# Two blocks of a transformer on one core: which modulation slabs TensorE multiplies directly

## The chip, the cores and the metric

The kernel runs on one core of one Trainium2 chip. The metric is the device time of one execution in microseconds (us), the median of several runs. The core has five engines, each with its own in-order instruction stream: TensorE (PE in the rows, with its weight loads as PEld), VectorE (DVE), ScalarE (ACT), GpSimd (POOL) and SyncE (SP). SP issues most of the DMAs here, one after the other.

## The reference, cut to what matters

Two transformer blocks follow each other on 512 tokens of width 1024. Only the start of the first block matters for the change: a condition vector `c` is turned into six modulation vectors by the matrix `w_ada` (1024 x 6144, float32), the tokens are normalised, scaled and shifted by the first two of them, and multiplied by `w_in`.

```
mod = silu(c) @ w_ada[l] + b_ada[l]
shift1, scale1, gate1, shift2, scale2, gate2 = split(mod, 6)
h = rms_norm(x, norm1_g[l]) * (1.0 + scale1) + shift1
z = h @ w_in[l]
c_q, c_kv, k_pe, dq, dk, dv = split(z, offsets)
```

What comes after is two kinds of attention (low-rank "mla" heads and differential heads), an output projection, a mixture of 32 experts, and then the second block: a convolution, sparse attention, cross attention and a feed-forward layer. The change touches none of these.

## The kernel before, in words

Products that need float32 accuracy are made of three matmuls (lines 84 to 86, the helper `mm3`): a matrix is split into a rounded high part and the low rest, and high x high, high x low and low x high are summed. A weight therefore passes through three steps: a DMA into a tile `raw`, a copy on ScalarE into `whi`, a subtraction on VectorE into `wlo` (line 100, or line 372 in the stage of the change).

**The start stage** (`phase_a1`, inside `tc.manual_schedule()`) runs in exactly the order in which it is written. The 512 tokens are normalised and transposed into `xT`, eight feature blocks of 128. Then the work comes in two halves of four feature blocks. For each half the kernel needs the matching 512 columns of shift1 and of scale1, that is `silu(c)` times a 1024 x 1024 part of `w_ada`. The class `Modulation` computes that from eight slabs of 128 rows and 1024 columns, 512 KB each. A slab can go one of two ways:

```
    def step(self):
        ...
        if k in self.direct:
            self.matmuls(w, g, k == ND - 1)
        elif k == 0:
            v.tensor_scalar(self.acc, w, g, None, op0=OP.mult)
        else:
            v.scalar_tensor_tensor(self.acc, w, g, self.acc, op0=OP.mult, op1=OP.add)
        if k == self.last:
            self.matmuls(self.acc, self.K.ones[:, 0:1], k == ND - 1)
```

On the VectorE way (lines 148 and 150) the slab is scaled by its part of `silu(c)` and added to the accumulator `acc`; once the last such slab is in, eight matmuls with a column of ones (line 137) sum `acc` over its rows. On the direct way the same eight matmuls of line 137 take the slab itself as weights and the column of `silu(c)` (`cs`) as the one moving column. Each of the eight float32 matmuls loads 128 x 128 weights, moves one column, and stands as two rows in the profile, so a slab or an accumulator makes 16 rows. All of them add into one PSUM tile `modb`, from which VectorE makes the factors `mod` (lines 377 and 379). ScalarE then scales and shifts `xT` into `hh` (lines 385 and 386), VectorE makes the rest `hl` (387), and TensorE multiplies with the slab of `w_in` (`products`, 48 matmuls for each half, into four PSUM tiles `pz`). In the first half slabs 1 and 4 are direct, in the second none.

The slabs of `w_ada` share eight buffers, so slab k of the second half is fetched into the buffer of slab k of the first half once that has been read. SP issues all DMAs in the written order; an issue that waits holds up everything behind it.

**After the start stage** the order is no longer the written one: a scheduler in the framework places the instructions of `a_proj` (the other columns of `w_in`, the rope products of line 229, and four more modulation vectors through `Gates.steps`, all on the VectorE way) and of the attention behind it on each engine. It does that with its own estimate of when each is ready, so a change in the start stage can shift the order there too.

Of the kernel before, what the change touches and what calls it, by code (L numbers as in the profile page):

```python
# [19 lines left out]
S, D, P = 512, 1024, 128  # L20
# [301 lines left out]
def phase_a1(K, pp, ps, pst, wp, pm, cols, gates):  # L322

    tc, nc, A = K.tc, K.nc, K.A
    T = {}
    w_in = A["w_in"][0]
# [11 lines left out]
    with tc.tile_pool(name="a_h", bufs=1, reuse_waits="tile") as ph:  # L338
        hh = ph.tile([P, ND, S], F32R, name="hh")
        hl = ph.tile([P, ND, S], F32R, name="hl")  # L340
        with tc.tile_pool(name="a_norm", bufs=1, reuse_waits="tile") as pn, tc.manual_schedule():
# [14 lines left out]
            def turned(t, x):  # L356
                for g in range(2):
                    pt = pst.tile([P, 4, P], F32, tag="tr", name=K.uid("tr"))
                    for j in range(4):
                        f = 4 * g + j  # L360
                        nc.tensor.transpose(pt[:, j, :], x[:, f * P:(f + 1) * P], K.ident)
                    nc.scalar.activation(xT[:, 4 * g:4 * g + 4, t * P:(t + 1) * P], pt, AF.Copy)

            def slab(n):
                raw = wp.tile([P, 4, 512], F32, tag="raw", bufs=2, name=K.uid("raw"))
                nc.sync.dma_start(raw, w_in[512 * n:512 * n + 512, 0:512].rearrange("(k p) c -> p k c", p=P))
                return (wp.tile([P, 4, 512], F32R, tag="whi", name=K.uid("whi")),
                        wp.tile([P, 4, 512], F32R, tag="wlo", name=K.uid("wlo")), raw)

            def part(w, k):  # L370
                nc.scalar.activation(w[0][:, k], w[2][:, k], AF.Copy)
                nc.vector.tensor_tensor(w[1][:, k], w[2][:, k], w[0][:, k].bitcast(F32), op=OP.subtract)
# [22 lines left out]
            wada = A["w_ada"][0].rearrange("r (s c) -> r s c", c=512)  # L395
            pz = [ps.tile([P, 512], F32, tag="sc" if t else "mm", name=K.uid("pz")) for t in range(NT)]
            xs = [scaled(0), scaled(1)]
            for t in range(NT):
                if t < 2:
                    xs.append(scaled(t + 2))  # L400
                turned(t, xs[t])
            mod = Modulation(K, pm, pm, ps, gates.cs, wada[:, 0:3:2], (1, 4))
            for k in range(ND):
                mod.step()
            w = slab(0)
            for k in range(3):
                part(w, k)
            m = factors(0, mod)
            part(w, 3)
            mod = Modulation(K, pm, pm, ps, gates.cs, wada[:, 1:4:2])  # L410
            for q in range(4):
                mod.step()
                modulated(0, q, m)
# [2 lines left out]
            for k in range(4):  # L416
                mod.step()
            products(0, 3, w)
            w = slab(1)
            for k in range(3):  # L420
                part(w, k)
# [5 lines left out]
            raw = wp.tile([P, ND, 2, 64], F32, tag="raw", bufs=2, name=K.uid("raw"))  # L427
# [9 lines left out]
        with tc.tile_pool(name="a_proj", bufs=2, reuse_waits="tile") as wk:  # L437
# [9 lines left out]
            for t in range(NT):  # L447
                for j in range(2):
                    c = slice(256 * j, 256 * j + 256)
# [145 lines left out]
def phase_a(K, R, ctx, st_b, dpool, modd):  # L595
    tc, nc, A = K.tc, K.nc, K.A
    with ExitStack() as st:
        ps = st.enter_context(tc.tile_pool(name="a_ps", bufs=3, space=PSUM))
        pst = st.enter_context(tc.tile_pool(name="a_pst", bufs=2, space=PSUM))
        with ExitStack() as sm:  # L600
            sq = ExitStack()
            with tc.tile_pool(name="a_pp", bufs=1) as pp:
                cols, cs = condition(K, pp, pst)
                lam_init = 0.8 - 0.6 * math.exp(-0.3 * 0)
                with tc.tile_pool(name="a_w", bufs=2, side="right", reuse_waits="tile") as wp:
                    with tc.tile_pool(name="a_mod", bufs=1, side="right", reuse_waits="tile") as pmod:
                        gates = Gates(K, pmod, ps, pst, cs, cols, modd)
                        T = phase_a1(K, pp, ps, pst, wp, pmod, cols, gates)
                    lam = mix_lambda(K, pp, lam_init)
                    pa = sq.enter_context(tc.tile_pool(name="a_qk", bufs=1, reuse_waits="tile"))  # L610
                    vecd = phase_up(K, T, pa, ps, wp, gates, dpool)
                pm = sm.enter_context(tc.tile_pool(name="a_mix", bufs=1, side="right", reuse_waits="tile"))
                mh = pm.tile([P, ND, S], F32R, name="mh")
                ml = pm.tile([P, ND, S], F32R, name="ml")
                router = router_weights(K, pm, ps)
                with tc.tile_pool(name="a_raw", bufs=1, side="right", reuse_waits="tile") as pr:
                    w_first = load_w(K, pm, A["w_out"][0], 0, 256, rawpool=pr, rawbufs=1, bufs=2)
                    phase_a2(K, T, mh, ml, ps, pst, lam, lam_init)
                sq.close()
# [1335 lines left out]
```

## Time and profile before

| | us |
|---|---|
| median of 3 runs | 1976.5 (1974.02 to 1979.04) |
| profiled execution | 1976.37 |
| its span, first to last instruction | 1974.6 |
| PE busy in it | 1908.5 (97%) |
| DVE busy | 1096.4 (56%) |
| ACT busy | 768.9 (39%) |
| mean DMA rate over the span | 181 GB/s |

The shares are means over stages with different limits. In the first 44 us, where the change is, PE is far from 97% busy and the DMA engines run at about 390 GB/s. The chain that ended last is PE work for 48% of the span, mostly the three matmuls of `mm3`.

### The profile page before, as it was taken

What the parts mean: (1) busy time and instruction counts of PE and PEld (TensorE: products, weight loads), DVE (VectorE), ACT (ScalarE), POOL (GpSimd) and SP (SyncE); (2) the same over time, 40 slices, a digit from 0 to 9 for tenths busy, and PEclk for the clock granted to TensorE, in tenths of its full rate; (3) what the DMA queues carried; (4) which work ended last, traced back from release to release, by engine and by line L of the source; (5) the groups of instructions that cost most, each with busy time, mean ns of one, the idle gap of its engine ahead of it and who ended that gap; (6) DMA issues with size and microseconds to landing.
All of it is one profiled execution on the core that took longest, in us unless ns stands there. A gap on an engine that the chain in (4) does not pass through costs nothing.

```text
span 1974.6 us, 26494 instructions
## 1 busy us (share of the span) xinstructions
PE 1908.5 (97%) x10338; PEld 1395.7 (71%) x10338; DVE 1096.4 (56%) x1963; ACT 768.9 (39%) x1602; POOL 148.7 (8%) x215
## 2 busy tenths in 40 slices
PE   6998998899999999979999999999999999999998
PEld 5786678545445454448777777777898898888886
DVE  6976653732332223356999989747555544444423
ACT  5435653321112211123336776786344443333321
POOL 0110000000000000001011001101100001111000
PEclk8999999899999999989999999999999999999999
DMA  9845045699999999953332222202342133333322
GB/s 309 313 170 144 1 179 191 236 408 403 420 415 416 416 420 415 399 155 100 96 107 64 55 54 65 54 22 75 96 130 85 44 91 96 100 96 97 126 78 86
DMA packets 212919, 356.89 MB, mean 181 GB/s; under 512 B 18519, under 2 KB 163283, under 8 KB 188216
## 3 DMA queue, kind: packets, MB, share of 16 engines
q1 hardware_dynamic: 210432, 348.91, 49.2%
q0 software_dynamic: 2096, 6.17, 1.0%
q8 instruction: 83, 1.36, 0.3%
q14 instruction: 44, 0.36, 0.1%
q10 hardware_dynamic: 264, 0.10, 0.0%
HBM read 350.88 MB, written 9.49 MB: 183 GB/s over the span
## 4 chain that ended last, share of the span: by engine, by line
PE 48%; DVE 5%; issue 1%; ACT 1%; DMA 0%; POOL 0%; DVEq 0%; POOLq 0%; SPq 0%; ACTq 0%
PE pz L86 13%; PE pz L84 13%; PE pz L85 13%; PE po L1653 3%; PE tr L1647 2%; DVE cva L1472 2%; DVE wlo L100 1%; PE sc L1623 1%; PE sc L1624 1%; PE pm L934 1%; PE po L1638 0%; PE tr L1297 0%; DVE q L241 0%; DVE K L251 0%; DVE p L1626 0%
## 5 line engine op out<-in xcount | busy, mean ns | idle before, releaser
L84 PE MATMUL pz<-hh,whi 128*128 128x512 f32 x912 | 362.7, 398 | 1.3 <-DVE cblk L1366 0.8
L86 PE MATMUL pz<-hh,wlo 128*128 128x512 f32 x912 | 360.0, 395 | 0.8 <-DVE wlo L100 0.8
L85 PE MATMUL pz<-hl,whi 128*128 128x512 f32 x912 | 359.2, 394 | 0.0
L99 ACT ACTIVATE whi<-raw 128x1024 fp32r<-128x1024 f32 (+2 forms) x166 | 181.1, 1096 | 350.6 <-PE pz L85 265.7
L100 DVE TENSOR_TENSOR wlo<-raw,whi 128x1024 fp32r<-128x1024 f32 (+2 forms) x166 | 219.6, 1326 | 81.7 <-ACT whi L99 81.2
L1070 PE MATMUL eg<-ew,xg 128*64 128x512 f32 x1024 | 224.3, 593 | 0.0
L84 PEld LDWEIGHTS pz<-hh,whi 128*128 128x128 f32 x912 | 171.4, 188 | 37.8 <-issue 2.1
L86 PEld LDWEIGHTS pz<-hh,wlo 128*128 128x128 f32 x912 | 171.4, 188 | 37.2 <-issue 2.1
L85 PEld LDWEIGHTS pz<-hl,whi 128*128 128x128 f32 x912 | 171.4, 188 | 35.3 <-issue 2.5
L1472 DVE SCALAR_TENSOR_TENSOR cva<-cv,cvp,cva 128x512 f32<-128x512 f32 x240 | 179.1, 757 | 4.2
L1070 PEld LDWEIGHTS eg<-ew,xg 128*64 128x64 f32 x1024 | 72.7, 137 | 142.3 <-issue 137.0
L1102 PE MATMUL ey<-ew,hT 128*64 128x512 f32 x512 | 115.1, 603 | 0.7 <-ACT hT L1091 0.7
L1107 DVE TENSOR_TENSOR yg<-ey,gate 128x512 f32<-128x512 f32 x32 | 22.1, 691 | 125.6 <-PE ey L1102 123.7
L1102 PEld LDWEIGHTS ey<-ew,hT 128*64 128x64 f32 x512 | 35.7, 138 | 70.7 <-issue 68.9
L991 ACT ACTIVATE xg<-px,norm2s 128x128 f32<-128x128 f32 x128 | 48.1, 456 | 90.3 <-PE px L986 90.3
L1108 ACT ACTIVATE yh<-yg 128x512 fp32r<-128x512 f32 x32 | 20.2, 630 | 156.4 <-DVE yg L1107 156.4
L1628 ACT ACTIVATE p<-p,am 128x128 f32<-128x128 f32 (+3 forms) x128 | 71.0, 559 | 19.6 <-DVE am L1626 16.6
L1626 DVE CUSTOM_DVE_ANT_0 p<-sc,bias 128x128 f32<-128x128 f32 (+3 forms) x128 | 59.8, 486 | 29.7 <-PE sc L1624 19.0
L1644 ACT ACTIVATE p<-p,am 128x128 f32<-128x128 f32 (+3 forms) x128 | 64.1, 554 | 13.4 <-DVE am L1634 13.1
L84 PE MATMUL pz<-whi,gh 128*128 128x512 f32 x176 | 68.5, 389 | 0.0
L85 PE MATMUL pz<-wlo,gh 128*128 128x512 f32 x176 | 68.5, 389 | 0.0
L86 PE MATMUL pz<-whi,gl 128*128 128x512 f32 x176 | 68.5, 389 | 0.0
(487 smaller groups left out, 3572.4 us busy)
## 6 DMA issues: line engine op xcount, KB each, us to landing
ew<-in_w_expert_gate_dram SPq DMA_DIRECT2D x64, 1024.0 KB
ew<-in_w_expert_up_dram SPq DMA_DIRECT2D x64, 1024.0 KB
ew<-in_w_expert_down_dram SPq DMA_DIRECT2D x64, 1024.0 KB
raw<-in_w_in_dram SPq DMA_DIRECT2D x53, 512.0 KB
wada<-in_w_ada_dram SPq DMA_DIRECT2D x48, 512.0 KB
raw<-in_ffn_in_w_dram SPq DMA_DIRECT2D x44, 512.0 KB
raw<-in_ffn_out_w_dram SPq DMA_DIRECT2D x22, 512.0 KB
raw<-in_w_in_dram SPq DMA_DIRECT2D x8, 1024.0 KB
```

The costliest lines, as they stand in the source:

```text
L84: nc.tensor.matmul(out, wh, hh, start=first, stop=False, **kw)
L85: nc.tensor.matmul(out, wh, hl, start=False, stop=False, **kw)
L86: nc.tensor.matmul(out, wl, hh, start=False, stop=last, **kw)
L99: nc.scalar.activation(hi[:, r], raw[:, r], AF.Copy)
L100: nc.vector.tensor_tensor(lo[:, r], raw[:, r], hi[:, r].bitcast(F32), op=OP.subtract)
L1070: nc.tensor.matmul(self.pz[64 * i:64 * i + 64], self.xg[:, k, 64 * i:64 * i + 64], next(self.rows_[i]), start=(k == 0), stop=(k == ND - 1))
L1102: nc.tensor.matmul(pys[c][64 * i:64 * i + 64], self.hT[:, k, 64 * i:64 * i + 64], wr[i][:, 512 * c:512 * c + 512], start=(k == 0), stop=(k ...
L1472: v.scalar_tensor_tensor(acc, cv[:, j:j + S], cvp[:, c, j:j + 1], acc, op0=OP.mult, op1=OP.add)
L1626: v.tensor_tensor_reduce(p, sc[:, :n], bt[r][:, b0:b0 + n], scale=1.0, scalar=3e38, op0=OP.add, op1=OP.min, accum_out=m[:, 0, b, i:i + 1])
L1628: nc.scalar.activation(p, p, AF.Exp, scale=-1.0, bias=m[:, 0, b, i:i + 1], accum_out=m[:, 1, b, i:i + 1])
L1644: nc.scalar.activation(p, p, AF.Copy, scale=m[:, 1, b, i:i + 1])
L1653: nc.tensor.matmul(po[64 * i:64 * i + 64, ts_], V[b][:, k, 64 * g:64 * g + 64], pts[i][:, k, :], start=False, stop=(b == 1 and k == t and ...
```

## The change

In the first half four slabs of `w_ada` instead of two are direct: 1, 3, 6 and 7 instead of 1 and 4. In the second half one is (slab 4) instead of none. The two slabs of `w_in` (1 MB each) are fetched by two DMAs of 512 KB each instead of one.

```diff
             def slab(n):
                 raw = wp.tile([P, 4, 512], F32, tag="raw", bufs=2, name=K.uid("raw"))
-                nc.sync.dma_start(raw, w_in[512 * n:512 * n + 512, 0:512].rearrange("(k p) c -> p k c", p=P))
+                for k in range(0, 4, 2):
+                    r = 512 * n + P * k
+                    nc.sync.dma_start(raw[:, k:k + 2], w_in[r:r + 2 * P, 0:512].rearrange("(k p) c -> p k c", p=P))
...
-            mod = Modulation(K, pm, pm, ps, gates.cs, wada[:, 0:3:2], (1, 4))
+            mod = Modulation(K, pm, pm, ps, gates.cs, wada[:, 0:3:2], (1, 3, 6, 7))
...
-            mod = Modulation(K, pm, pm, ps, gates.cs, wada[:, 1:4:2])
+            mod = Modulation(K, pm, pm, ps, gates.cs, wada[:, 1:4:2], (4,))
```

Three places in the program's order carry the prediction. The lines of the changed kernel are two higher from line 367 on, and its buffer numbers are higher too. The first is PE at the start. Before, `acc` is the last thing that `modb` sums:

```order
L361 MATMUL tr_212<-ident,xt_141 128x128 x4
L137 MATMUL modb_224<-cs,wada_222 128x1 x8
L137 MATMUL modb_224<-cs,wada_239 128x1 x8
L137 MATMUL modb_224<-ones,acc_218 128x1 x8
L84 MATMUL pz_142<-whi_268,hh 128x512
```

Now:

```order
L361 MATMUL tr_212<-ident,xt_141 128x128 x4
L137 MATMUL modb_224<-cs,wada_222 128x1 x8
L137 MATMUL modb_224<-cs,wada_236 128x1 x8
L137 MATMUL modb_224<-ones,acc_218 128x1 x8
L137 MATMUL modb_224<-cs,wada_260 128x1 x8
L137 MATMUL modb_224<-cs,wada_270 128x1 x8
L84 MATMUL pz_142<-whi_283,hh 128x512
```

Two more direct slabs stand between the sum of `acc` and the first product. In the second half PE likewise has one direct slab (`wada` slab 4) ahead of the sum of `acc`, behind the products of the first three feature blocks.

The second place is VectorE in `a_proj`, at the end of shift2, the second of the four vectors (`acc_674` before, `acc_697` now). Before:

```order
L150 SCALAR_TENSOR_TENSOR acc_674<-wada_766,cs,acc_674 128x1024
L80 SCALAR_TENSOR_TENSOR dq_115<-rx_612,dq_114 128x512
L150 SCALAR_TENSOR_TENSOR acc_674<-wada_769,cs,acc_674 128x1024
L148 TENSOR_SCALAR acc_785<-wada_786,cs 128x1024
L150 SCALAR_TENSOR_TENSOR acc_674<-wada_772,cs,acc_674 128x1024
L150 SCALAR_TENSOR_TENSOR acc_785<-wada_789,cs,acc_785 128x1024
L100 TENSOR_TENSOR wlo_795<-raw_792,whi_794 128x2048
L231 TENSOR_TENSOR ry_757<-pr_755,sinT 128x512
L178 TENSOR_TENSOR norm_64<-modb_775,cols 128x8
L233 TENSOR_TENSOR rx_718<-rx_718,ry_757 128x512
```

Now:

```order
L150 SCALAR_TENSOR_TENSOR acc_697<-wada_786,cs,acc_697 128x1024
L80 SCALAR_TENSOR_TENSOR dq_115<-rx_635,dq_114 128x512
L150 SCALAR_TENSOR_TENSOR acc_697<-wada_789,cs,acc_697 128x1024
L148 TENSOR_SCALAR acc_808<-wada_809,cs 128x1024
L150 SCALAR_TENSOR_TENSOR acc_697<-wada_792,cs,acc_697 128x1024
L150 SCALAR_TENSOR_TENSOR acc_808<-wada_812,cs,acc_808 128x1024
L150 SCALAR_TENSOR_TENSOR acc_697<-wada_795,cs,acc_697 128x1024
L231 TENSOR_TENSOR ry_780<-pr_778,sinT 128x512
L178 TENSOR_TENSOR norm_64<-modb_798,cols 128x8
L233 TENSOR_TENSOR rx_741<-rx_741,ry_780 128x512
L100 TENSOR_TENSOR wlo_818<-raw_815,whi_817 128x2048
```

The vector is complete one step later, and the weight rest `wlo` (line 100) stands behind line 178, which reads the `modb` of that vector. On PE, before:

```order
L229 MATMUL pr_755<-rx_718,rot 128x512
L137 MATMUL modb_775<-ones,acc_674 128x1 x8
L84 MATMUL pz_798<-hh,whi_794 128x512
L85 MATMUL pz_798<-hl,whi_794 128x512
L86 MATMUL pz_798<-hh,wlo_795 128x512
```

Now, with work of other tiles (line 551 is line 549 of before, the scores of a differential head) ahead of the first use of `wlo`:

```order
L229 MATMUL pr_778<-rx_741,rot 128x512
L137 MATMUL modb_798<-ones,acc_697 128x1 x8
L84 MATMUL pz_821<-hh,whi_817 128x512
L85 MATMUL pz_821<-hl,whi_817 128x512
L229 MATMUL pr_848<-rx_776,rot 128x512
L84 MATMUL pz_856<-hh,whi_817 128x512
L85 MATMUL pz_856<-hl,whi_817 128x512
L551 MATMUL sc_1550<-dk_120,dq_112 128x512
L551 MATMUL sc_1551<-dk_120,dq_112 128x512
L551 MATMUL sc_1575<-dk_120,dq_112 128x512
L86 MATMUL pz_821<-hh,wlo_818 128x512
```

The third place is one set of weights later: the sum of scale2 (`acc_785` before, `acc_808` now). Before, its last slab is scaled ahead of lines 100 and 231 on VectorE:

```order
L150 SCALAR_TENSOR_TENSOR acc_785<-wada_883,cs,acc_785 128x1024
L80 SCALAR_TENSOR_TENSOR dk_123<-rx_753,dk_122 128x512
L100 TENSOR_TENSOR wlo_907<-raw_904,whi_906 128x2048
L231 TENSOR_TENSOR ry_862<-pr_860,sinT 128x512
L178 TENSOR_TENSOR norm_64<-modb_886,cols 128x8
```

Now it is scaled behind them:

```order
L100 TENSOR_TENSOR wlo_930<-raw_927,whi_929 128x2048
L231 TENSOR_TENSOR ry_885<-pr_883,sinT 128x512
L150 SCALAR_TENSOR_TENSOR acc_808<-wada_906,cs,acc_808 128x1024
L233 TENSOR_TENSOR rx_846<-rx_846,ry_885 128x512
L178 TENSOR_TENSOR norm_64<-modb_909,cols 128x8
```

Line 231 reads the rope product `pr` of the same place on PE. There, before:

```order
L86 MATMUL pz_833<-hh,wlo_795 128x512
L229 MATMUL pr_860<-rx_823,rot 128x512
L137 MATMUL modb_886<-ones,acc_785 128x1 x8
L84 MATMUL pz_910<-hh,whi_906 128x512
L85 MATMUL pz_910<-hl,whi_906 128x512
```

Now:

```order
L229 MATMUL pr_883<-rx_846,rot 128x512
L551 MATMUL sc_1550<-dk_121,dq_112 128x512
L551 MATMUL sc_1551<-dk_121,dq_112 128x512
L551 MATMUL sc_1550<-dk_120,dq_113 128x512
L551 MATMUL sc_1551<-dk_120,dq_113 128x512
L551 MATMUL sc_1575<-dk_121,dq_112 128x512
L551 MATMUL sc_1575<-dk_120,dq_113 128x512
L137 MATMUL modb_909<-ones,acc_808 128x1 x8
L84 MATMUL pz_933<-hh,whi_929 128x512
```

Six score products now stand between the rope product and the sum.

## Rows read from the trace of the kernel before

**Rows 1.** Stretches: length, busy PE, PEld, DVE, ACT, POOL, granted PE clock, DMA share, GB/s

```profile
20.00:24.00 4.00, 1.30 (x11) 1.25 (x11) 3.35 (x3) 0.00 (x0) 0.00 (x0) 0.69 1.05 387
24.00:28.00 4.00, 3.18 (x15) 3.10 (x15) 2.46 (x6) 2.42 (x5) 0.00 (x0) 0.50 1.05 387
40.00:44.00 4.00, 3.79 (x25) 3.14 (x24) 3.44 (x7) 2.23 (x5) 0.00 (x0) 1.00 0.40 141
92.00:102.00 10.00, 10.00 (x48) 8.02 (x48) 9.42 (x11) 2.79 (x3) 3.66 (x2) 1.00 1.03 385
162.00:172.00 10.00, 7.57 (x33) 5.89 (x33) 6.82 (x14) 5.91 (x12) 0.30 (x1) 0.98 1.03 280
```

**Rows 2.** Timeline of PE in the start stage: start us, us, instructions, [idle before]

```profile
17.31 3.63 PE L137 MATMUL modb<-cs,wada 128*128 128x1 f32 x32
23.64 3.54 PE L137 MATMUL modb<-ones,acc 128*128 128x1 f32 x16 [2.70 <-DVE acc L150]
28.64 0.80 PE L84 MATMUL pz<-whi,hh 128*128 128x512 f32 x1 [1.46 <-ACT hh L385]
40.77 1.95 PE L137 MATMUL modb<-ones,acc 128*128 128x1 f32 x16 [0.21 <-DVE acc L150]
42.57 0.48 PE L84 MATMUL pz<-whi,hh 128*128 128x512 f32 x1
```

**Rows 3.** Timeline of DVE in the start stage

```profile
16.83 6.66 DVE L150 SCALAR_TENSOR_TENSOR acc<-wada,cs,acc 128x1024 f32<-128x1024 f32 x5
27.32 0.16 DVE L377 TENSOR_TENSOR mod<-modb,cols 128x8 f32<-128x8 f32 x1
35.47 5.24 DVE L150 SCALAR_TENSOR_TENSOR acc<-wada,cs,acc 128x1024 f32<-128x1024 f32 x4
```

**Rows 4.** Stretches as in rows 1: the clock's fall, and two busy stretches

```profile
21.00:21.50 0.50, 0.00 (x0) 0.00 (x0) 0.50 (x1) 0.00 (x0) 0.00 (x0) 0.98 1.07 393
21.50:22.00 0.50, 0.00 (x0) 0.00 (x0) 0.50 (x1) 0.00 (x0) 0.00 (x0) 0.50 1.04 385
...
17.50:21.50 4.00, 3.44 (x31) 3.35 (x31) 3.84 (x4) 0.61 (x2) 0.00 (x0) 1.00 1.05 387
219.00:223.00 4.00, 3.26 (x17) 2.24 (x15) 2.54 (x9) 2.10 (x12) 1.19 (x2) 1.00 0.01 2
223.00:227.00 4.00, 4.00 (x20) 2.09 (x18) 3.24 (x7) 3.26 (x8) 0.00 (x0) 1.00 0.00 0
```

**Rows 5.** Timeline of ACT in the start stage

```profile
24.85 2.19 ACT L371 ACTIVATE whi<-raw 128x512 fp32r<-128x512 f32 x4 [6.74 <-DMA raw<-in_w_in_dram]
27.77 0.82 ACT L385 ACTIVATE hh<-xT,mod 128x512 fp32r<-128x512 f32 x1 [0.73 <-DVE mod L379]
```

**Rows 6.** Waits of SP's DMA queue, 0 to 60 us: us in total, times, longest

```profile
SPq L94 <- DVE wlo L372: 3.8, 1, 3.8
```

**Rows 7.** Timeline of DVE, 88 to 94 us

```profile
88.27 2.46 DVE L150 SCALAR_TENSOR_TENSOR acc<-wada,cs,acc 128x1024 f32<-128x1024 f32 x2
90.66 2.27 DVE L100 TENSOR_TENSOR wlo<-raw,whi 128x2048 fp32r<-128x2048 f32 x1
93.46 0.14 DVE L178 TENSOR_TENSOR norm<-modb,cols 128x8 f32<-128x8 f32 x1
```

**Rows 8.** Timeline of PE, 90 to 110 us

```profile
90.61 1.02 PE L229 MATMUL pr<-rx,rot 128*128 128x512 f32 x2
91.47 1.84 PE L137 MATMUL modb<-ones,acc 128*128 128x1 f32 x16
93.17 0.48 PE L84 MATMUL pz<-hh,whi 128*128 128x512 f32 x1
93.71 0.40 PE L86 MATMUL pz<-hh,wlo 128*128 128x512 f32 x1
108.51 0.73 PE L549 MATMUL sc<-dk,dq 64*128 64x512 f32 x4
109.18 0.50 PE L86 MATMUL pz<-hh,wlo 128*128 128x512 f32 x1
```

## The prediction

> **What bounds the kernel now.** I read the stretches first, then the timelines of the engines in them, then the waits. From about 44 us on PE has work without a break: ten-microsecond stretches show 10.00 us of it, as 92 to 102 [rows 1], until the first real gap near 168 us (7.57 of 10 us busy there). So whatever delays PE before 44 us moves the rest, unless something later waits for a resource that did not move; none does, since SP issues the later loads in order and its first one after the stage waits 3.8 us for a VectorE step that needs the second half's factors [rows 6]. The DMA gap in 40 to 44 us (141 GB/s against 387 before it) is that wait.
>
> In the start stage the reader should see two chains. In the first half PE multiplies two direct slabs from 17.31 to 20.94 [rows 2], that is 1.82 us a slab, stands idle, and then sums `acc` from 23.64 to 27.18, 3.54 us for half as many rows. VectorE feeds `acc` with five steps over 6.66 us, 1.33 each [rows 3]. The factors follow at 27.32, `hh` at 27.77 [rows 5], the first product at 28.64. The second half ends with a sum at 40.77, which waited only 0.21 us for `acc`, and products again from 42.57.
>
> The reason for 3.54 against 1.82 is the granted clock: it falls from 2.4 to 1.2 GHz at about 21.5 us [rows 4] and is still at 0.50 in 24 to 28 us [rows 1]. What PE did just before is the point: from 17.5 to 21.5 it was busy 3.44 of 4 us, with one-column matmuls, and the clock fell. From 219 to 223 it was busy less, 3.26 of 4 us, with wide matmuls, and the clock stayed at 1.00 after it. I read this as: one-column matmuls do not hold the clock.
>
> **The change part by part.**
>
> *First half.* VectorE loses two of five steps, so `acc` is ready at 16.83 + 3 x 1.33 = 20.8 us instead of 23.5. PE gets two more direct slabs. Slabs 1 and 3 keep it busy to 20.94; then come the sum, slab 6 and slab 7, three groups of 16 rows. The slabs have landed by then: VectorE started slab 6 at about 20.8 and slab 7 at 16.83 + 4 x 1.33 = 22.2 before. With the clock falling at 21.5 again, 0.55 us of the first group run at full rate, 0.3 of a group; the other 2.7 groups take 2.7 x 3.54 = 9.55 us. `modb` ends at 31.05 instead of 27.18: +3.9 us. Bounds: all three at full rate, 20.95 + 3 x 1.82 = 26.4, is -0.8; all at half rate, and the slab before them too (1.7 more), is 20.95 + 10.6 + 1.7 = 33.3, or +6.1. I take +3.9, the clock's fall where the row shows it. The products of the first three feature blocks then start 3.9 us later with a slow clock, as they did before; I assume as many slow ones (one us of uncertainty).
>
> *Second half.* VectorE loses one step of 1.31 us (5.24 over 4 [rows 3]), PE gets 16 rows more ahead of the sum. PE sets the end here (the wait was 0.21 us), so the slab costs its full 42.57 - 40.77 = 1.8 us, and the 0.2 us wait goes: +1.6 us. It could only be less if PE were early enough to wait for `acc`, which is the rival below.
>
> *The slabs of `w_in` in two pieces.* Their first conversion could begin when the first 512 KB are there, about 1.35 us (512 KB at 387 GB/s) before the 24.85 us of [rows 5]. ScalarE ended its four pieces at 27.04, 0.7 us ahead of `hh`; with the factors at 31 the pieces are hidden whole, and in the second half, with the factors near 48, the more so. Value 0; two more issues on SP cost nothing while the DMA engines have a full queue (387 GB/s in 20 to 28 us [rows 1]).
>
> *The queue behind the direct slabs.* The second half's slabs 6 and 7 reuse buffers that PE now frees at about 27.5 and 31 us instead of VectorE at 22 and 23.5. Behind them on SP wait the second `w_in` slab, the k_pe weights and the rope tables. Slabs 0 to 5 are in the queue behind the `w_in` slab that landed at 24.85 [rows 5]; at 1.35 us each they land until 33, so the engines do not run dry, and VectorE wants slab 7 after 40: value 0, at most 1 us.
>
> *The shifted order in `a_proj`.* This is a cost by itself. I count in times of before, without the shift. VectorE is nearly full there (9.42 of 10 us in 92 to 102 [rows 1]), and it now brings in one slab more right before the sum of shift2. The two steps at 88.27 take 2.46 us [rows 7]; a third takes the place of line 100 at 90.66, so `acc` is ready at 91.9 instead of 89.5. PE's sum starts at 92.2 instead of 91.47 [rows 8] and line 84 follows 1.70 later at 93.9. Line 178 waits for that sum, about 94.2; line 233 behind it takes 0.65 and line 100 then 2.2 us, so `wlo` is ready at 97.2 to 97.3. Line 86 needed it at 93.71 before: 3.6 us later. PE fills part of that with a rope product (0.86, from 90.61 to 91.47), two matmuls (0.23 each) and three score products (0.168 each, four from 108.51 to 109.18): 1.8 us that it saves later.
>
> From there 44 matmuls of 0.2335 us take PE to 107.6 and the next rope product to 108.5 (its result at 108.6). Line 231 (0.6) and the last slab of scale2 (1.25) follow on VectorE, so the sum can start at 110.65; the six score products cover only one us of that, PE idles 1.2. Line 84 is at 112.35 and line 86, 0.64 behind it, at 113.0 instead of 109.18: 3.8 us. Five score products more are done by then (0.85), the rest has evened out: +3.0 us. Bounds: 0, if VectorE has slack that I don't see, and 3.8, if the scores done ahead save nothing because the gap near 168 us swallows them. I take 3.0.
>
> Sum: 3.9 + 1.6 + 3.0 = 8.5 us on the profiled execution of 1976.37 (span 1974.6, 1.8 around it), which is the median of the runs (1976.5): **1984.9 us**.
>
> **The rivals.**
>
> *The clock holds.* If PE's unbroken work from 17.3 us on keeps the full clock, `modb` ends at 26.4 (-0.8). The products then run at 0.23 us each: `hh` 0.8 earlier, 36 products end near 37, the direct slab at 38.7. `acc` is ready at 40.7 - 0.8 - 1.3 = 38.6, and the sum ends at 40.55 instead of 42.57: -2.0 us. With the order's 3.0 that is +1.0: 1977.4, no change. It decides from the point where the clock stays at 1.00 through 22 to 26 us. For it speaks that PE had idled 0.55 us before the fall; against it, the two busy stretches of [rows 4]. The Trainium skill, "TensorE: Matmul & The Clock Gate", section "Why this matters for your kernels", advises keeping TensorE continuously busy to have the full clock, with no idle gaps between bursts of matmuls; by that rule this rival would be the forecast, 1977.4, and by the rows 1984.9. The trace disagrees as far as it goes: a stretch that was 86% busy ended in a fall.
>
> *The order costs nothing.* VectorE makes up the steps and only the start stage counts: +5.5, 1981.9. For it: before, line 86 followed line 84 by only 0.54 us [rows 8], so there was no wait at that place. Against it: line 178 reads what PE sums, and the order on each engine is fixed.
>
> *Both at once.* The clock holds and the order is free: -2.0, 1974.4, what the change saves when nothing speaks against it, and still no change by the measure below. It needs both conditions, so it is the least likely.
>
> **How the numbers follow.** A difference under 0.3%, 5.9 us, cannot be told from none here. Forecast 0.62, its own range 1981 to 1989; the order costs nothing 0.17; the clock holds 0.13; both at once and what I don't see 0.08. Above 1982.4 lie nine tenths of the first, a third of the second, a quarter of the last: 0.64. Below 1970.6 I leave 0.05, for later gaps in which the clock may now fall less often; 0.31 for no change. The range 1977 to 1989 takes in half of the clock's case and all of the order's.
>
> **What would show it.** Right: `modb` of the first half ending near 31 us with a granted clock of 0.50 from about 21.5, the first product near 32.5, the first product after the second sum near 48; a wait of PE for line 100 and one for line 150 between 95 and 125 us. Wrong: a clock of 1.00 through 22 to 28 us, or line 86 behind shift2's sum at once. If the first half costs what I say and the total moves less than 5 us, the gap near 168 us has taken it back.

## The result, and the profile after

The changed kernel takes 1987.5 us, the median of 4 runs (1986.76 to 1989.3); the kernel before took 1977.5 beside it. The ratio is 1.0053, 95% interval 1.0041 to 1.0065, so 8.1 to 12.9 us slower, about 10.5. The prediction was 1984.9 with a range of 1977 to 1989.

| | us |
|---|---|
| profiled execution | 1987.19 |
| its span | 1985.5 (+10.9) |
| PE busy | 1921.8 (+13.3) |
| DVE busy | 1093.5 (-2.9) |
| mean DMA rate over the span | 180 GB/s |

PE got three groups of 16 rows more, 5.5 us at the full clock ([rows 2]: 1.82 each), and was busy 13.3 us longer: part of its work ran at the lower clock. The first view to read is PE's timeline in the start stage, against [rows 2] (lines are two higher from line 367 on):

```profile
17.74 4.83 PE L137 MATMUL modb<-cs,wada 128*128 128x1 f32 x32
22.43 3.55 PE L137 MATMUL modb<-ones,acc 128*128 128x1 f32 x16
25.84 6.97 PE L137 MATMUL modb<-cs,wada 128*128 128x1 f32 x32
34.16 0.80 PE L84 MATMUL pz<-whi,hh 128*128 128x512 f32 x1 [1.36 <-ACT hh L387]
...
45.80 1.84 PE L137 MATMUL modb<-cs,wada 128*128 128x1 f32 x16
47.50 1.93 PE L137 MATMUL modb<-ones,acc 128*128 128x1 f32 x16
49.29 0.48 PE L84 MATMUL pz<-whi,hh 128*128 128x512 f32 x1
```

The five groups of the first half follow each other without a gap, and the last three take 3.5 us each; `modb` ends at 32.8 instead of 27.2. The first product after the second sum comes at 49.29, 6.7 us later than in [rows 2]. The stretches say why (columns as in [rows 1]):

```profile
19.50:20.00 0.50, 0.50 (x6) 0.50 (x5) 0.44 (x2) 0.00 (x0) 0.00 (x0) 0.93 1.05 385
20.00:20.50 0.50, 0.50 (x4) 0.50 (x4) 0.50 (x1) 0.00 (x0) 0.00 (x0) 0.50 1.06 389
20.00:24.00 4.00, 4.00 (x21) 4.00 (x20) 1.25 (x1) 0.03 (x1) 0.00 (x0) 0.50 1.05 387
24.00:28.00 4.00, 4.00 (x21) 4.00 (x20) 1.99 (x3) 2.26 (x4) 0.00 (x0) 0.50 1.05 386
...
50.50:51.00 0.50, 0.50 (x3) 0.36 (x2) 0.00 (x0) 0.47 (x2) 0.00 (x0) 0.65 0.00 0
51.00:51.50 0.50, 0.50 (x3) 0.40 (x2) 0.00 (x0) 0.50 (x2) 0.00 (x0) 0.50 0.00 0
...
92.00:102.00 10.00, 9.65 (x49) 7.46 (x48) 8.72 (x10) 3.63 (x4) 1.35 (x1) 1.00 0.82 278
122.00:126.00 4.00, 4.00 (x11) 3.04 (x11) 3.23 (x5) 1.03 (x1) 0.00 (x0) 0.57 0.03 12
```

PE is busy for 4.00 of 4 us, and the granted clock is 0.50 all the same. It fell near 19.9 us, 1.6 us earlier than in [rows 4], and by 126 us twice more, near 50.7 and 122. The VectorE that set the end of the first half before now waits for PE, for 6.16 us:

```profile
32.84 0.17 DVE L379 TENSOR_TENSOR mod<-modb,cols 128x8 f32<-128x8 f32 x1 [6.16 <-PE modb L137]
...
49.47 0.17 DVE L379 TENSOR_TENSOR mod<-modb,cols 128x8 f32<-128x8 f32 x1 [2.75 <-PE modb L137]
```

The pieces do what they say: ScalarE starts 0.9 us before [rows 5], with a short wait for the second piece, and nobody needs it by then:

```profile
23.97 1.15 ACT L373 ACTIVATE whi<-raw 128x512 fp32r<-128x512 f32 x2 [5.43 <-DMA raw<-in_w_in_dram]
25.32 1.15 ACT L373 ACTIVATE whi<-raw 128x512 fp32r<-128x512 f32 x2 [0.21 <-DMA raw<-in_w_in_dram]
```

SP's queue (waits from 0 to 60 us: total, times, longest) now waits for PE to free the direct slabs' buffers, and for line 374 5.9 us longer than in [rows 6]. It cost PE nothing that can be seen: no product of the stage waits for a DMA.

```profile
SPq L143 <- PE modb L137: 12.7, 4, 5.3
SPq L94 <- DVE wlo L374: 9.7, 1, 9.7
```

In `a_proj` PE shows both waits that the prediction named, where [rows 8] had none:

```profile
100.33 1.95 PE L137 MATMUL modb<-ones,acc 128*128 128x1 f32 x16 [0.35 <-DVE acc L150]
...
105.34 0.50 PE L86 MATMUL pz<-hh,wlo 128*128 128x512 f32 x1 [0.52 <-DVE wlo L100]
...
116.66 1.19 PE L551 MATMUL sc<-dk,dq 64*128 64x512 f32 x6
120.01 1.95 PE L137 MATMUL modb<-ones,acc 128*128 128x1 f32 x16 [2.16 <-DVE acc L150]
```

**A ledger.** To see where time is lost, I compare the start of the same instruction in two traces. A column is one kernel's start minus that of the kernel before, in us, good to about 0.1; all but the first are experiments, told below.

| at (us before), line | after | pieces | direct | direct, 64 col. | after, 64 col. | slab 0, pieces | slabs 0, 4 |
|---|---|---|---|---|---|---|---|
| 54.5, L444 | +8.4 | -0.6 | +5.5 | +2.2 | +0.1 | +0.9 | -1.4 |
| 110.7, L200 | +15.3 | +6.4 | +5.5 | +3.0 | +8.8 | +8.8 | -0.5 |
| 147.3, L1334 | +14.6 | +5.3 | +5.5 | +3.7 | +8.1 | +8.3 | -0.3 |
| 266.4, L557 | +11.8 | +2.5 | +3.6 | +2.4 | +8.9 | +7.7 | -2.3 |
| 866.7, L1122 | +12.1 | +2.5 | +1.5 | +1.2 | +8.8 | +6.8 | -2.3 |
| 874.6, L1424 | +8.8 | +2.5 | -1.9 | -2.2 | +5.5 | +3.4 | -5.6 |
| 1967.3, L1883 | +10.9 | +2.8 | -1.1 | -1.9 | +5.5 | +3.7 | -5.7 |
| ratio of times | 1.0053 | 1.0030 | 1.0013 | 0.9991 | 1.0028 | 1.0023 | 0.9970 |

In the changed kernel 8.4 us are lost by 54 us and 6.9 more by 111; then 0.7 come back by 147, 2.8 by 266 and 3.3 in one step near 870; 1.9 are lost near 1460. The ledger is one execution each and the ratios are medians of up to 12, so the last two rows differ by a few us.

### The profile page after: what moved, and what is told of

Same layout as the page of the kernel before. It is cut to its first block, busy times and chain, and to the rows that moved or that the text cites. A ratio compares the mean times of both kernels' runs of the same rounds, so it can differ in the third digit from the quotient of the medians.

```text
span 1985.5 us, 26591 instructions
## 1 busy us (share of the span) xinstructions
PE 1921.8 (97%) x10386; PEld 1407.7 (71%) x10386; DVE 1093.5 (55%) x1960; ACT 768.8 (39%) x1602; POOL 150.3 (8%) x215
## 3 DMA queue, kind: packets, MB, share of 16 engines
q8 instruction: 83, 1.36, 0.3%
## 4 chain that ended last, share of the span: by engine, by line
PE 47%; DVE 5%; issue 1%; ACT 1%; DMA 0%; POOL 0%; POOLq 0%; DVEq 0%; SPq 0%; ACTq 0%
PE pz L86 12%; PE pz L84 12%; PE pz L85 12%; PE po L1655 3%; PE tr L1649 2%; DVE cva L1474 2%; DVE wlo L100 1%; PE sc L1625 1%; PE sc L1626 1%; PE pm L936 1%; DMA xkr<-xkd 0%; PE po L1640 0%; PE tr L1299 0%; DVE q L241 0%; DVE K L251 0%
## 5 line engine op out<-in xcount | busy, mean ns | idle before, releaser
L1628 DVE CUSTOM_DVE_ANT_0 p<-sc,bias 128x128 f32<-128x128 f32 (+3 forms) x128 | 59.9, 486 | 29.8 <-PE sc L1626 19.1
```

Of the source, the lines that this page charges most:

```text
L1628: v.tensor_tensor_reduce(p, sc[:, :n], bt[r][:, b0:b0 + n], scale=1.0, scalar=3e38, op0=OP.add, op1=OP.min, accum_out=m[:, 0, b, i:i + 1])
```

## The experiments

My theory was that two costs add up: the direct slabs, made dear by the clock, and the shifted order. Rivals: the order carries it all or nothing; width has nothing to do with the clock; the DMA queue behind the direct slabs. The two parts of the change separate them: with the pieces alone the order of the changed kernel appears in `a_proj`, with the direct sets alone that of the kernel before stays. From 188.6 us of the kernel before on, the two orders are the same on every engine. No run has the changed order without the DMA that brings it.

**Pieces alone, direct sets alone.** Each is one half of the diff above.

> The kernel before with only the two-piece fetch of the w_in slabs (direct slabs as before: 1 and 4, none). Its order after the start stage is the changed kernel's. Theory (the shifted order is a cost by itself, worth 3 to 4 us): the start stage as before (modb of the first half ends at 27.2, first product after the second sum at 42.6), then PE waits for line 100 and line 150 near 97 and 117 us; total +3 to +4 us, ratio 1.0015 to 1.002. Rival A (the order is free, all comes from the direct slabs): within 1 us of before. Rival B (the order costs what the ledger lost in a_proj, 5 us, and nothing is given back): +5.

> The kernel before with only the direct sets of the change (1, 3, 6, 7 and 4), slabs of w_in in one piece. Its order after the start stage is that of before. Theory (one-column matmuls let the clock fall, and each direct slab costs PE 1.8 us warm and 3.5 us cold): first sum ends near 32.8 us, first product after the second sum +6.7 us, the clock falls again near 51 us for another 1.6 us, no wait for line 150 near 117 us; total +5 to +8 us, ratio 1.0025 to 1.004. Rival A (the order carries it): within 2 us of before. Rival B (it is the queue, since the direct slabs hold SP until 33 us): the same total, but then the waits in front of the first products of a_proj are for DMAs.

Measured: pieces 1.0030 (1.0019 to 1.0041), direct sets 1.0013 (1.0002 to 1.0023). The pieces alone cost 3.8 to 8.1 us, more than expected, though their start stage is 0.6 us early. PE's timeline shows the waits, VectorE's the step that PE waits for, and the stretches a fall of the clock behind it:

```profile
91.41 1.95 PE L137 MATMUL modb<-ones,acc 128*128 128x1 f32 x16 [0.36 <-DVE acc L150]
...
96.42 0.51 PE L86 MATMUL pz<-hh,wlo 128*128 128x512 f32 x1 [0.50 <-DVE wlo L100]
...
111.09 1.95 PE L137 MATMUL modb<-ones,acc 128*128 128x1 f32 x16 [2.15 <-DVE acc L150]
```

```profile
109.35 1.69 DVE L150 SCALAR_TENSOR_TENSOR acc<-wada,cs,acc 128x1024 f32<-128x1024 f32 x1
```

```profile
112.00:113.00 1.00, 1.00 (x11) 1.00 (x11) 0.00 (x0) 1.00 (x2) 0.00 (x0) 1.00 0.20 82
113.00:114.00 1.00, 1.00 (x4) 0.82 (x4) 0.92 (x2) 1.00 (x1) 0.00 (x0) 0.51 0.06 25
114.00:115.00 1.00, 1.00 (x3) 0.80 (x3) 1.00 (x3) 0.11 (x1) 0.00 (x0) 0.50 0.00 0
```

The direct sets alone cost 0.4 to 4.5 us, less than the 5 to 8 expected. Their trace holds its 5.5 us from 54 to 159 us without a change: with the order of before nothing is lost in `a_proj`. The clock fell later than in the changed kernel, within the sum, and, against the expectation, not near 50 us:

```profile
21.62 2.95 PE L137 MATMUL modb<-ones,acc 128*128 128x1 f32 x16 [0.54 <-DVE acc L150]
24.43 6.96 PE L137 MATMUL modb<-cs,wada 128*128 128x1 f32 x32
```

**Sixty-four equal columns, everywhere line 137 is used.**

```diff
-            self.K.nc.tensor.matmul(self.out[:, j:j + 1], w[:, j // 4, j % 4 * P:j % 4 * P + P], g,
+            self.K.nc.tensor.matmul(self.out[:, 64 * j:64 * j + 64], w[:, j // 4, j % 4 * P:j % 4 * P + P],
+                                    g.to_broadcast([P, 64]), ...
```

> The changed kernel with the moving column of line 137 repeated to 64 columns (each matmul writes 64 equal columns of modb, of which one is read); everything else the same. Theory (matmuls that move one column do not hold the clock, wider ones do): the clock stays at 1.00 from 20 to 32 us, the five groups of the first half follow each other at about 1.8 us each and end near 26.5 us instead of 32.8, no fall near 51 and 122 us; the second half is about 7 us earlier; total 6 to 8 us under the changed kernel, 1979 to 1981.5. Rival (the clock falls for another reason, the weight loads or the slab waits, and width does not matter): clock 0.50 from 20 us as before, groups of 3.5 us, total within 1.5 us of the changed kernel. A middle case: the clock holds, but 64 columns cost 0.03 us a row more (64/512 of 0.2335), 0.5 us a group, so 3 us of the gain go.

> The kernel before with the moving column of line 137 repeated to 64 columns. Theory (width holds the clock): the sum of the first half takes about 1.8 us instead of 3.54 and modb ends near 25.5; the 36 products after it run at 0.23 us where they now run at half clock until 36 us; but PE sets the end of the start stage only if acc of the second half is there in time (it waits for VectorE, which gains no more than 1.7 us), so the total falls by 1 to 2 us. If the 2.7 us in which PE waits for acc let the clock fall anyway: within 0.5 us of before, with the fall at 21 to 24 us still there. Rival (width does not matter): the fall at 21.5 us as before.

Measured: the changed kernel so 1.0007 (0.9998 to 1.0015), `modb` of the first half ending at 26.7 with every group at about 1.8 us; the kernel before so 1.0008 (0.9997 to 1.0019), no gain. Its fall stayed, behind PE's wait for `acc`, and the 64-column sum took 3.65 us:

```profile
24.64 3.65 PE L137 MATMUL modb<-ones,acc 128*128 128x64 f32 x16 [3.30 <-DVE acc L150]
```

So a wait can let the clock fall whatever the width. These two totals are weak evidence: the width also went to the sums of `a_proj`, which moved the order in the attention. The next runs have 64 columns in the start stage alone, and there the order is exactly that of their twins.

**One column against 64 with no wait ahead.** Three direct slabs, `(4, 5, 6)`, in the second half of the kernel before, behind 36 products:

> The kernel before with three direct slabs in the second half (4, 5, 6), one column wide: four groups of 16 rows in a row, after 36 wide products at a full clock and without idle time ahead of them. It asks whether one-column matmuls alone let the clock fall. Theory: they do; the clock falls to 0.50 within or right behind the four groups, which take more than 4 x 1.8 = 7.2 us (9 to 12 us). Rival (only idle time lets it fall, as the 0.5 us ahead of the direct slabs of the first half): 7.2 us, clock 1.00 throughout.

> The same three direct slabs with 64 moving columns in the start stage. Theory: the clock stays at 1.00 through the four groups, 7.2 to 7.5 us. Rival (idle time, or the weight loads, whatever the width): the same times and clock as with one column.

PE's timeline and the stretches with one column:

```profile
40.31 5.53 PE L137 MATMUL modb<-cs,wada 128*128 128x1 f32 x48
45.70 3.55 PE L137 MATMUL modb<-ones,acc 128*128 128x1 f32 x16
```

```profile
40.50:45.00 4.50, 4.50 (x42) 4.50 (x42) 1.68 (x3) 1.31 (x3) 0.00 (x0) 1.00 0.32 114
45.00:45.50 0.50, 0.50 (x7) 0.50 (x6) 0.00 (x0) 0.00 (x0) 0.00 (x0) 0.96 0.00 0
45.50:49.00 3.50, 3.50 (x19) 3.50 (x18) 0.00 (x0) 0.00 (x0) 0.00 (x0) 0.50 0.00 0
```

and with 64:

```profile
39.10 5.47 PE L137 MATMUL modb<-cs,wada 128*128 128x64 f32 x48
44.41 1.95 PE L137 MATMUL modb<-ones,acc 128*128 128x64 f32 x16
```

PE was busy without a break in both. With one column the clock fell near 45.5 us, at the end of the third group, and the fourth took 3.55 us; with 64 it stayed. The four groups took 8.8 and 7.1 us. These are one execution each, but the other traces agree. Seven of them have five or six groups of 64 columns in a row, 9 to 11 us with waits of at most 0.4 us, and the clock is at 1.00 over all of them; the seven falls that start stages with 64 columns have came in or right behind waits of PE of 0.8 to 3.3 us. Behind one-column groups it fell near 50.7 us of the changed kernel too, with no wait ahead. So idle time is not needed for a fall: one-column groups can bring it, and none of 64 columns did without a wait. The Trainium skill, "TensorE: Matmul & The Clock Gate", section "Why this matters for your kernels", advises to keep TensorE continuously busy for the full clock. Of the waits the runs agree with it (24.64 above); here PE was busy for 3.50 of 3.50 us at 0.50, and the advice alone does not save such a stretch.

**The change's direct sets with 64 columns in the start stage**, slabs of `w_in` in one piece, and then in two (which is the changed kernel with 64 columns):

```diff
-            mod = Modulation(K, pm, pm, ps, gates.cs, wada[:, 0:3:2], (1, 4))
+            mod = Modulation(K, pm, pm, ps, gates.cs, wada[:, 0:3:2], (1, 3, 6, 7), 64)
...
-            mod = Modulation(K, pm, pm, ps, gates.cs, wada[:, 1:4:2])
+            mod = Modulation(K, pm, pm, ps, gates.cs, wada[:, 1:4:2], (4,), 64)
```

> The kernel before with the change's direct sets (1, 3, 6, 7 and 4), slabs of w_in in one piece, and the moving column repeated to 64 columns in the start stage alone; the order after it is that of before. It differs from the run with the direct sets alone only in the width. Theory (one-column matmuls let the clock fall, 64 columns hold it): the first half's five groups at 1.8 us each, factors 4 to 5 us earlier than with one column (L377 near 27 to 28 instead of 31.4), first product after the second sum near 43, within 1 us of before; 5 us less than with one column at 135 us. Total within 2 us of before, about 2 us under the one-column version, since part of any early delay is given back near 170 and 870 us. Rival (the direct slabs cost PE as much whatever the width): first product after the second sum near 48, total +2 to +3 us.

> The changed kernel with 64 moving columns in the start stage alone; every engine's order is the changed kernel's. Theory (the clock and the order are two separate costs): the start stage ends like that of before (first product after the second sum near 42.5 instead of 49.3), the order's waits in a_proj stay (PE waits for lines 100 and 150), and at 147 us the kernel is 5 to 6 us behind the kernel before instead of 14.6. Total 6 to 8 us under the changed kernel, 1979 to 1982, ratio to before 1.001 to 1.003. Rival (an earlier start only makes PE wait longer in a_proj, so little is left): 1985 or more.

Measured: 0.9991 (0.9982 to 0.9999) and 1.0028 (1.0015 to 1.0041). Against their one-column twins the width gains 0.22% and 0.25%, 4 to 5 us. The first of the two ends its start stage 2.1 us late, where at most 1 was expected: the clock fell at 29.8 us, behind PE's wait for `hh`. The changed kernel's start stage is then back at that of before (+0.1 at 54.5 us):

```profile
20.47 1.97 PE L137 MATMUL modb<-ones,acc 128*128 128x64 f32 x16
22.27 3.74 PE L137 MATMUL modb<-cs,wada 128*128 128x64 f32 x32
```

Yet 8.7 us are lost between 54 and 111 us, and at 147 us the kernel is 8.1 behind, not the 5 to 6 expected. PE still waits for line 150 (0.36 and 1.36 us), no longer for line 100, and the clock falls twice, 95 to 99 and 112 to 119 us, which costs half of that time, 5.1 us. The order's cost doesn't hang on the late start, but here the clock behind the waits is the larger part of it.

**A version to beat both, and the order once more.** Direct slabs 1, 3, 6, 7 and, in the second half, slab 0, which PE can multiply while it waits for `hh`; 64 columns; and only the first slab of `w_in` in two pieces, which leaves the order of before:

```diff
-        elif k == 0:
+        elif k == self.lead:
...
+                e = 4 if n else 2
+                for k in range(0, 4, e):
+                    r = 512 * n + P * k
+                    nc.sync.dma_start(raw[:, k:k + e], w_in[r:r + e * P, 0:512].rearrange("(k p) c -> p k c", p=P))
...
+            mod = Modulation(K, pm, pm, ps, gates.cs, wada[:, 1:4:2], (0,), 64)
```

> A version meant to beat both: first half direct 1, 3, 6, 7; second half direct slab 0 (it fills PE while it waits for the first hh) instead of 4; 64 moving columns in the start stage; only the first slab of w_in in two pieces, which leaves the order after the start stage as before. Theory: modb of the first half near 26.6 us, slab 0 to 28.4, then 36 products of 0.23 us with no fall of the clock, acc ready near 38.8, first product after the second sum near 40.6, 2 us earlier than before; total -1 to -3 us. If the clock falls near 29 us all the same (1.7 us): near 42, total within 1 us of before. If slab 0 has not landed by 26.6: 1 us later.

> The twin of the run before: the version meant to beat both, with the first slab of w_in in two pieces alone. Timed again beside its twin, since its first interval reached from -0.2 to +0.1%. Theory: start stage 1 to 2 us ahead of the kernel before, total -1 to -4 us. Rival (what is won at the start is absorbed later): within 1 us of before.

> The version meant to beat both (direct 1, 3, 6, 7 and 0, 64 columns in the start stage) with both slabs of w_in in two pieces instead of the first alone: one more DMA on SP, and with it the changed kernel's order in a_proj. Theory (the order is the cost, not the DMA): the same start stage to 0.3 us, then 5 to 6 us lost between 90 and 125 us, of which some 2.7 come back near 170 us; total +3 to +6 us against its twin of this call. Rival (the order is free): within 1 us of the twin. Should a_proj's VectorE now have slack, since the start is 7 us earlier than in the changed kernel: +1 to +2.

Measured: 0.9998 (0.9981 to 1.0014), again 0.9993 (0.9980 to 1.0005), and with both slabs in two pieces 1.0023 (1.0007 to 1.0039). The version itself could not be told from the kernel before: PE waited 2.24 us for `acc` ahead of the second sum, and in the second of the runs the clock fell there. Its twin shows the order's cost again, 0.30% (5.9 us), and the same waits. Giving slab 4 of the second half to PE as well, `(0, 4)`, fills that wait:

> The version meant to beat both, with slab 4 of the second half direct as well as slab 0, so that PE no longer waits 2.24 us for acc there. Theory (what is left of the clock's falls in the start stage comes behind PE's waits): PE multiplies slab 4 from about 37.7 to 39.4, sums acc without a wait, first product after the second sum near 41 us, no fall of the clock between 36 and 46 us; total -1 to -4 us against before. Rival (the wait was harmless, slab 4 is only work added to PE): as its version without slab 4, -1 to -3 us, or up to 1 us slower than it.

Measured: **1970.3 us, ratio 0.9970 (0.9958 to 0.9981)**, faster than both and more than the 1 to 4 us expected. From 17.6 us on the start stage has no wait of PE over 0.63 us, and the clock is full to 108 us; PE's timeline and one stretch:

```profile
23.08 5.52 PE L137 MATMUL modb<-cs,wada 128*128 128x64 f32 x48
29.75 0.50 PE L86 MATMUL pz<-whi,hl 128*128 128x512 f32 x1 [0.63 <-DVE hl L393]
37.65 1.89 PE L137 MATMUL modb<-cs,wada 128*128 128x64 f32 x16
39.38 1.95 PE L137 MATMUL modb<-ones,acc 128*128 128x64 f32 x16
```

```profile
36.00:46.00 10.00, 10.00 (x61) 8.83 (x61) 6.74 (x11) 6.30 (x10) 0.00 (x0) 1.00 0.84 224
```

Of its 5.7 us in the ledger only 1.4 are the start stage. A fall of the clock at 108 us takes 1.1 us back; 2.0 come between 147 and 266 us and 3.3 in the step near 870.

## Why the prediction came out

The direction and the mechanisms were right; the sizes were off, and that the total came so near is in part luck. By 147 us the changed kernel had lost 14.6 us, not the 8.5 of the sum, and 3.7 came back later for reasons that the sum doesn't hold.

- *First half, +3.9.* Right: the direct sets alone show +4.1 at the first factors (27.3 us before). Two misses cancel in it: `acc` let the sum start only at 21.62 instead of 20.95 us, and the clock fell 0.8 us later than at 21.5. In the changed kernel the fall came 1.6 us earlier, at 19.9, and it was +5.5, within the bound of 6.1.
- *Second half, +1.6.* Right as work: the slab took 1.7 us, and the direct sets alone go from +4.1 to +5.5 over it, 1.4. Its other cost was not in the sum: in the changed kernel the clock fell behind the two one-column groups, and 1.7 more us went by 54.5 (6.7 to 8.4). In the run with the direct sets alone it didn't. The same work has a fall in one execution and none in another.
- *Pieces, 0, and the queue, 0.* Right for the transfers. What I hadn't asked is where the shifted order comes from: it is the second slab's second DMA, so the part that I priced at nothing carries the dearer term.
- *Order, +3.0: the step that was mis-sized.* From 54.5 to 147.3 us the four kernels of the ledger with the changed order lose 5.9, 6.2, 8.0 and 7.4 us (pieces, after, after with 64 columns, slab 0 with pieces), and the times of the pairs differ by 0.30 to 0.40%, 5.9 to 7.9 us. PE's idle time was right in sum and not in its parts: in the run with the pieces PE idles 0.86 us at place 2 and 2.15 at place 3, 3.0 in all, where the prediction had 1.8 and 1.2. Line 86 of place 2 came at 96.42, which is 97.0 counted from the kernel before's start (forecast 97.3). At place 3 the step of line 150 took 1.69 us, not 1.25; why, no run shows. The sum behind it started at 111.67 on that count instead of 110.65. The prediction took off the five score products done ahead, 0.8 us, which the ledger still holds at 147 us. What it put at nothing is the clock behind the waits: it was at 0.50 from 113 to about 116.4, which costs half of that, 1.7. 3.0 + 0.8 + 1.7 is 5.5 of the 5.9. In the other three the lower clock costs 1.7, 5.1 and 3.4 us of the same stretch. All four with the changed order have such a fall there; of the eight kernels with the order of before two have one, of 1.7 us, right behind a one-column sum of `a_proj` and without a wait (slabs 0 and 4 at 108 us, direct sets with 64 columns at 112).
- *"So whatever delays PE moves the rest": wrong, and so is the doubt that the gap near 168 us takes it back.* That gap is still there in the changed kernel, later and 0.5 us shorter. Here it is before and after, and then the stretch from 147 to 266 us of before with the same work in the changed kernel:

```profile
171.00 0.50 PE L84 MATMUL pz<-cnh,whi 128*128 128x512 f32 x1 [2.43 <-DVE mql L80]
184.47 0.50 PE L84 MATMUL pz<-cnh,whi 128*128 128x512 f32 x1 [1.92 <-DVE mql L80]
```

```profile
147.30:266.40 119.10, 110.23 (x547) 76.60 (x547) 82.38 (x180) 68.73 (x172) 7.27 (x10) 0.96 0.21 60
161.90:278.20 116.30, 108.02 (x542) 75.50 (x542) 82.15 (x180) 68.59 (x172) 7.29 (x10) 0.97 0.22 62
```

Of the 2.8 us that come back here 0.8 are the five score products done ahead (547 PE rows against 542), 0.6 less idle time (8.9 against 8.3 us), and the rest the clock, at 0.50 for 10.2 us before and for 6.8 now, worth 1.7. The direct sets alone, in the order of before, have the same 6.8 and get 1.9 back. That the delay spares this fall is not shown. The gap near 870 us became 3.4 us shorter, for a reason of its own (below). Against it stands a wait of PE of 1.6 us near 1460 us, which the kernel before doesn't have; six of the fourteen traces have one there, 0.8 to 1.6 us, and its cause stays open:

```profile
1458.00:1463.00 5.00, 3.39 (x29) 3.11 (x28) 5.00 (x5) 4.93 (x10) 0.00 (x0) 1.00 0.10 25
```

Of the rivals, "the clock holds" is refuted by the stretches, "the order costs nothing" by the pieces alone. The latter had the direct sets' 5.5 us right as well, and even these end as 2.5 us (0.13%) in the times, 4.5 (0.23%) beside the pieces.

## What to carry to other kernels

Moving work to the matrix engine is priced at the clock that it leaves behind, not only at its own duration: one-column matmuls cost 1.8 us a group at the full clock and 3.5 at half, and the wide matmuls behind them pay too. Repeating the moving column to 64 cost at most 0.05 us a group and, in the start stage, kept the clock wherever PE did not wait. And where a scheduler places the later work, compare the order on each engine for every part of a change alone: here the split of a DMA, harmless in its own stage, cost through the order of the next one 0.30 to 0.40%, and the work that was moved 0.13 to 0.23%.

## What the hardware showed that I had not expected

- The clock's falls are partly chance. The two profiles of the version with slab 0 are of one program: in the one the clock was full at the second sum (2.00 us), in the other it fell there (2.66 us), and they end 2.4 us apart. Terms under 2 us are better read from a ledger ahead of such a fall than from totals.
- PE's gap in front of line 1424 (line 1426 now) goes with the number of instructions that PE has. With 10338 matmul rows (the kernel before, the pieces alone, the kernel before with 64 columns) it is 7.8 to 7.9 us, with 10386 or 10402 (the other eleven) 4.6 to 4.7. Here are the kernel before and the changed one:

```profile
874.58 1.07 PE L1424 MATMUL tr<-ident,cvrows 34*128 34x34 f32 x8 [7.93 <-DMA raw<-in_w_in_dram]
```

```profile
883.37 1.07 PE L1426 MATMUL tr<-ident,cvrows 34*128 34x34 f32 x8 [4.57 <-POOL cv L1451]
```

The releaser named for the first can't be meant: in the changed kernel the same transfer is issued 0.2 us before PE goes on. PE's weight loads show 8.37 and 5.0 us there with no releaser at all. The records of PE's own sequencer show where the time goes: in the loop of line 1127 (line 1129 now) it takes the same 13 semaphore steps in 5.0 us before and in 1.7 us now:

```profile
L1127 PEldq EVENT_SEMAPHORE  x13: 51/51/51, 869.1 to 874.1; - x13
L1129 PEldq EVENT_SEMAPHORE  x13: 51/51/51, 881.3 to 883.0; - x13
```

In the three kernels with the longer gap it stands still once for 3.3 to 3.7 us; in the eleven no step of it there takes over 0.7. The other engines are through the same steps by 871.1 us in the kernel before, so it is not one of them that PE waits for. In all fourteen the queues that the trace calls instruction queues load 16 KB and twice 8 KB in this gap. A wait of the sequencer for its instructions would fit, but no run shows it. The shorter gap gives some 3.3 us to every kernel here that has more direct slabs than the kernel before, so more than half of the fastest version's 5.7 us in the ledger has nothing to do with the reason for which the slabs were moved.
